# The output stage of a recurrent layer in two parts, and a scheduling priority for mixes and clamps

## The chip, the cores and the metric

The kernel runs on one core of a Trainium2 chip. The metric is the device time of one execution in microseconds (us), the median of several runs. One core has five engines that take their instructions in order, each from its own stream: TensorE (PE: matrix products and transposes; its weight loads, PEld, are listed apart), VectorE (DVE), ScalarE (ACT), GpSimd (POOL) and SyncE (SP, which issues transfers). They wait for each other by semaphores. Products are written to PSUM tiles; the other tiles lie in SBUF.

## The reference

Two layers over 2048 tokens of width 1024, in float32. Each layer normalises its input, projects it, runs one token mixer and one small cross-attention to 256 memory tokens, multiplies both by a SiLU gate, projects back and adds. The first layer's mixer is the one at issue here, a recurrence (RWKV-7) over 12 heads of width 64:

```python
z = z + (token_shift(z) - z) * mu
r, k, v, wd, ad = jnp.split(z, ...)
...
def step(state, inp):
    r_t, w_t, k_t, v_t, kk_t, a_t = inp
    sa = jnp.einsum('bhvk,bhk->bhv', state, -kk_t)
    state = state * w_t + sa * (kk_t * a_t) + v_t * k_t
    y_t = jnp.einsum('bhvk,bhk->bhv', state, r_t)
...
y = ((y - mean) * lax.rsqrt(var + LNX_EPS)) * lnx_w + lnx_b
y = (y + bonus) * silu(gate)
```

(The broadcasts are left out.) The second layer is a differential attention over all tokens, which takes the rest of the time and which the change does not touch.

## The kernel before

**Tiling.** The first layer (`layer_a`) works in steps. A step takes two heads (128 channels, one of 6 pairs) and a block of 512 tokens (8 chunks of 64). With 6 pairs and 4 blocks there are 24 steps; they run in two halves of the sequence, two blocks to a pair's weights. Within a step the recurrence is solved chunk by chunk, with a triangular inverse.

**The stages of a step** (class `Step`):

- `p1`: the projections of k, r and v (`pj`, 24 products each of 128x512), the low-rank decay and rate (`lr`, 4 products), each followed by ScalarE and VectorE work. `mix` (L274 to L279) forms the token shift out of a projection's PSUM bank: a scaled copy on ScalarE, two multiply-adds on VectorE (L277, L278), and a copy of the last column to `carry` (L279). The clamps (L320 for decay and rate) keep an exponential finite. `pss` (L335) sums the squared keys over a head; it needs kx's projection, its mix, kk (L331) and rn (L333).
- `p2`: the masked score matrices (`pg` into `Gm`, L371 and L373), transposes of keys and values (`bkp`, `pvt`), the bonus.
- `p3`: on VectorE, the inverse of 16x16 blocks (30 small operations, L418 and L420), then two block transposes that give T16 (L427) and TT16 (L431).
- `p3b`: the inverse of 64x64 blocks on TensorE: two sets of 32 small products `inv` (L446), the first from E1 and T16, the second from ScalarE's copy of the first (L448) and TT16; then L449 and a block transpose Ta (L452) on VectorE, `invz` (L459), a copy on ScalarE (L461), `invr` (L465), and copies on VectorE (L467).
- `p4`: `atp`, `nvp`, `txp`, `mrp` and `ch`, products with copies on ScalarE between them.
- `p4b`: the chain over the 8 chunks: one product `ch` and one ScalarE copy S for each chunk (L541, L542), with the outputs `yp`, copied to `ys` (L557).
- `p5`: the output stage: statistics and normalisation of `ys` on VectorE (L564 to L575), four transposes `py` on TensorE (L578), a scaled copy on ScalarE (L580), the bonus added on VectorE (L581), the gate multiplied on GpSimd (L582), and a store to `y_dram` on GpSimd's own queue (L583).
- `gate`: the gate's projection and its SiLU (`gate_silu`, L281 to L289), with a clamp on VectorE (L285).

**The order written in the loop.** For step i: p2 and p3 of step i+1, p4b and p5 of step i, p3b and p4 of step i+1, then `filler(i + 2)`, which is the gate of step i+1 and p1 of step i+2, with the loads of weights where they are due.

**What makes the order on an engine.** The order in which the code issues instructions is their rank, not their order. A scheduler places each instruction at build time, by its own estimates of durations: whenever an engine is free, it gives it the instruction of highest rank among those that are ready. The streams that come out are fixed; at run time each engine takes its own in order and waits where the estimate was too short. The projections of the next step, issued last, are so the filling between the products of the current step. `tc.high_priority()` gives what is issued inside it a rank ahead of everything else.

**PSUM.** `ppj` has 3 banks, tag `pj`, for projections, `lr`, `pss` and `pbn`. `pps` has 3 banks, tag `gm`, that serve `pg`, `bkp`, `pvt`, `yp`, `py`, `inv`, `invz`, `invr`, `atp`, `nvp`, `txp` and `mrp` in turn, and 2 for `ch`.

Of the kernel before, what the change touches and what calls it, by code (L numbers as in the profile page):

```python
# [11 lines left out]
ALU = mybir.AluOpType  # L12
# [13 lines left out]
TB = 512  # L26
# [10 lines left out]
BIG = float(2.0 ** 60)  # L37
# [22 lines left out]
def hybrid_kernel(ctx, tc, S, HALF, x, mem, pv, cv, dist, postn, w_out, w_mkv, a_w, w2, a2, w_kv, b_w, out):  # L60
# [4 lines left out]
    V = nc.vector  # L65
# [143 lines left out]
    def layer_a(ph):  # L209
# [43 lines left out]
        def PS(shape, name, tag="gm", bufs=3):  # L253
            if tag == "pj":
                return ppj.tile(shape, F32, name=name, tag="pj", bufs=3)
            return pps.tile(shape, F32, name=name, tag=tag, bufs=bufs)
# [17 lines left out]
        def mix(ps, col, o):  # L274
            m = pc("mu", col)
            A.activation(o, ps, AF.Copy, scale=omu[:, col:col + 1])
            V.scalar_tensor_tensor(out=o[:, 1:TB], in0=ps[:, 0:TB - 1], scalar=m, in1=o[:, 1:TB], op0=ALU.mult, op1=ALU.add)  # L277
            V.scalar_tensor_tensor(out=o[:, 0:1], in0=carry[:, col:col + 1], scalar=m, in1=o[:, 0:1], op0=ALU.mult, op1=ALU.add)  # L278
            V.tensor_copy(out=carry[:, col:col + 1], in_=ps[:, TB - 1:TB])  # L279

        def gate_silu(ps, g, eng=G_):  # L281
            A.activation(g, ps, AF.Copy)  # L282
            e = W([P, TB], "e_sil")
            A.activation(e, g, AF.Exp, scale=-1.0)
            V.tensor_scalar(out=e, in0=e, scalar1=BIG, scalar2=None, op0=ALU.min)  # L285
            A.activation(e, e, AF.Ln, bias=1.0)
            A.activation(e, e, AF.Exp, scale=-1.0)
            eng.tensor_tensor(out=g, in0=g, in1=e, op=ALU.mult)
            return g  # L289
# [13 lines left out]
        class Step:  # L303
# [5 lines left out]
            def p1(self):  # L309
                p, h, th, ws = self.p, self.h, self.th, self.ws  # L310
                lora = self.lora
                cum = W([P, NC, 65], "cum")
                asg = W([P, TB], "asg")
                G_.memset(cum[:, :, 0:1], 0.0)
                for i, e in enumerate((cum[:, :, 1:65], asg.rearrange("p (c t) -> p c t", t=C))):
                    pl = PS([P, TB], "lr", "pj")
                    mm(pl, lhsT=lora[:, i], rhs=th[i], start=True, stop=False)
                    mm(pl, lhsT=lora[:, 2 + i], rhs=th[i], start=False, stop=True)
                    A.activation(e, pl.rearrange("p (c t) -> p c t", t=C), AF.Exp, bias=nwa[:, i * 6 + p:i * 6 + p + 1], scale=-1.0)
                    V.tensor_scalar(out=e, in0=e, scalar1=BIG, scalar2=None, op0=ALU.min)  # L320
                    A.activation(e, e, AF.Ln, bias=1.0)
                    A.activation(e, e, AF.Exp, scale=-1.0)
                kx = W([P, TB], "kx")
                mix(pj(ws[0], h), 6 + p, kx)
                cumf = cum.rearrange("p c t -> p (c t)")
                V.tensor_tensor_scan(cumf, cc("smask", NC * 65), cumf, 0.0, op0=ALU.mult, op1=ALU.add)
                Pt = W([P, NC, 65], "Pt")
                A.activation(Pt, cum, AF.Exp, scale=-DEC)
                A.activation(cum, cum, AF.Exp, scale=DEC)
                kk = W([P, TB], "kk")  # L330
                V.tensor_scalar(out=kk, in0=kx, scalar1=pc("k_k", p), scalar2=None, op0=ALU.mult)  # L331
                rn = W([P, TB], "rn")
                A.activation(rn, kk, AF.Square)  # L333
                pss = PS([P, TB], "pss", "pj")
                mm(pss, lhsT=bones, rhs=rn, start=True, stop=True)  # L335
                V.tensor_scalar(out=rn, in0=pss, scalar1=1e-12, scalar2=None, op0=ALU.max)
                A.activation(rn, rn, AF.Ln)
                A.activation(rn, rn, AF.Exp, scale=-1.0)
                G_.tensor_tensor(out=rn, in0=rn, in1=asg, op=ALU.mult)

                AR = T([P, NC, P], "AR", 2)
                BK = TL([P, NC, P], "BK", 1)
                Pt4 = Pt.rearrange("p (j e) t -> p j e t", e=2)
                Pi4 = cum.rearrange("p (j e) t -> p j e t", e=2)[:, :, :, 1:65]
                V.tensor_tensor(out=slots(AR, True), in0=q4(kk), in1=Pt4[:, :, :, 0:64], op=ALU.mult)
                G_.tensor_tensor(out=kk, in0=kk, in1=rn, op=ALU.mult)
                V.tensor_tensor(out=slots(BK, True), in0=q4(kk), in1=Pi4, op=ALU.mult)

                V.tensor_scalar(out=asg, in0=asg, scalar1=pc("k_a", p), scalar2=oka[:, p:p + 1], op0=ALU.mult, op1=ALU.add)
                G_.tensor_tensor(out=kx, in0=kx, in1=asg, op=ALU.mult)  # L350
                V.tensor_tensor(out=slots(BK, False), in0=q4(kx), in1=Pi4, op=ALU.mult)
                PC = T([P, NC], "PC", 3)
                V.tensor_copy(out=PC, in_=Pt[:, :, 64])
                rx = W([P, TB], "rx")
                mix(pj(ws[1], h), p, rx)
                V.tensor_tensor(out=slots(AR, False), in0=q4(rx), in1=Pt4[:, :, :, 1:65], op=ALU.mult)
                G_.tensor_tensor(out=kx, in0=rx, in1=kx, op=ALU.mult)
                vx = W([P, TB], "vx")
                mix(pj(ws[2], h), 12 + p, vx)
                self.rk, self.AR, self.BK, self.PC, self.vx = kx, AR, BK, PC, vx  # L360

# [195 lines left out]
                    A.activation(ys[:, :, hh], py[hh], AF.Copy)  # L557

            def p5(self):
                p, ys, sil = self.p, self.ys, self.sil  # L560
                bs = T([P, 8, 6], "bs", 1)
                y8 = ys.rearrange("p j h v -> p (j h) v")
                for i in range(8):
                    V.bn_stats(out=bs[:, i, :], in_=y8[:, i, :])  # L564
                sm = T([P, 4, 8], "sm", 1)
                V.tensor_tensor(out=sm[:, 0], in0=bs[:, :, 1], in1=bs[:, :, 4], op=ALU.add)
                V.tensor_tensor(out=sm[:, 1], in0=bs[:, :, 1], in1=bs[:, :, 4], op=ALU.subtract)
                V.tensor_tensor(out=sm[:, 2], in0=bs[:, :, 2], in1=bs[:, :, 5], op=ALU.add)
                V.scalar_tensor_tensor(out=sm[:, 3], in0=sm[:, 1], scalar=16.0, in1=sm[:, 1], op0=ALU.mult, op1=ALU.mult)
                V.tensor_tensor(out=sm[:, 2], in0=sm[:, 2], in1=sm[:, 3], op=ALU.add)  # L570
                V.tensor_scalar(out=sm[:, 0], in0=sm[:, 0], scalar1=0.5, scalar2=None, op0=ALU.mult)
                A.activation(sm[:, 3], sm[:, 2], AF.Ln, bias=eps_t[:, 1:2], scale=1.0 / 64)
                A.activation(sm[:, 3], sm[:, 3], AF.Exp, scale=-0.5)
                V.tensor_tensor(out=y8, in0=y8, in1=sm[:, 0, :, None].broadcast_to([P, 8, 64]), op=ALU.subtract)
                V.tensor_tensor(out=y8, in0=y8, in1=sm[:, 3, :, None].broadcast_to([P, 8, 64]), op=ALU.mult)  # L575
                py = PS([P, NJ, P], "py")
                for j in range(NJ):
                    nc.tensor.transpose(py[:, j, :], ys[:, j].rearrange("p h v -> p (h v)"), ident)  # L578
                yo = ys.rearrange("p j h v -> p (j h v)")
                A.activation(yo, py.rearrange("p j t -> p (j t)"), AF.Identity, bias=pc("lnx_b", p), scale=pc("lnx_w", p))  # L580
                V.tensor_tensor(out=yo, in0=yo, in1=self.bon, op=ALU.add)  # L581
                G_.tensor_tensor(out=yo, in0=yo, in1=sil, op=ALU.mult)  # L582
                G_.dma_start(out=y_dram[p * P:(p + 1) * P, self.t0:self.t0 + TB], in_=yo)  # L583
# [109 lines left out]
        for i in range(n):  # L693
            if i + 1 < n:
                steps[i + 1].p2()
                steps[i + 1].p3()
            steps[i].p4b()
            if i == n - 1:
                load_wo(0)
                for m in range(2):  # L700
                    mem_q(m, NHALF - 1, [NB - 1], ws[m])
                stl.close()
                op = OutProj(0, y_dram, x, x1_dram, 3)
            steps[i].p5()
            if i + 1 < n:
                steps[i + 1].p3b()
                steps[i + 1].p4()
            if i + 2 <= n:
                filler(i + 2)
            if i == n - 2:  # L710
                ws = [mem_w(m) for m in range(2)]
                for m in range(2):
                    mem_q(m, NHALF - 1, range(NB - 1), ws[m])
# [610 lines left out]
```

## Time and profile before

| | us |
|---|---|
| median of 3 runs | 3177.18 (3177.15 to 3179.72) |
| the profiled execution | 3178.13 |
| its span, first to last instruction | 3176.3 |
| TensorE busy | 2965.9 (93% of the span) |
| VectorE busy | 1792.0 (56%) |
| ScalarE busy | 1508.2 (47%) |
| GpSimd busy | 873.6 (28%) |

The span holds the whole program; 1.8 us of the profiled execution lie outside it. The busy shares are means over both layers. The first layer's steps end at some 1500 us. Of the rows further down, those of the order of time give the start, the duration, the engine, the line, the operation and, in brackets, how long the engine stood idle before it and what released it. A row of matrix products shows how many are merged (x32), and a tile's name is cut at the first digit of its number, so that T16 reads T and TT16 reads TT.

### The profile page before, as it was taken

The numbers are of one execution on the slowest core, as the hardware profiler recorded it, in microseconds if no ns is written. First come the engines' busy times: TensorE is split into PE (matmuls) and PEld (weight loads), VectorE is DVE, ScalarE is ACT, GpSimd is POOL, SyncE is SP. The second block draws the span as 40 slices with busy tenths as digits, with TensorE's granted clock in tenths as the row PEclk, the third lists the DMA queues.
The fourth block names the chain that finished last, engine by engine and source line by source line (L and its number), as shares of the span: only waits on it lengthen the run. The fifth ranks groups of instructions, "written<-read, shape, count | busy, mean of one in ns | idle before, by whom it ended". The sixth has DMA issues, their size and how long they took to land.

```text
span 3176.3 us, 57448 instructions
## 1 busy us (share of the span) xinstructions
PE 2965.9 (93%) x22378; PEld 2401.6 (76%) x22378; DVE 1792.0 (56%) x4728; ACT 1508.2 (47%) x3318; POOL 873.6 (28%) x936
## 2 busy tenths in 40 slices
PE   6889999998789999998899999999999999998999
PEld 4667777776667777777677798898887787786777
DVE  6566767655656676764465311101108888887554
ACT  5535454444444544444455422313216777776343
POOL 3133433442134334431000222412312223222100
PEclk8999999998789999999999999999999999999999
DMA  3211000122110001103554523423454556533453
GB/s 118 80 30 36 28 23 26 35 77 79 36 33 28 23 26 33 38 25 86 164 145 126 155 80 99 118 83 87 117 158 110 114 112 120 116 80 108 121 156 115
DMA packets 266160, 265.45 MB, mean 84 GB/s; under 512 B 16832, under 2 KB 206656, under 8 KB 265760
## 3 DMA queue, kind: packets, MB, share of 16 engines
q1 hardware_dynamic: 237760, 195.31, 21.0%
q0 software_dynamic: 28128, 66.46, 10.3%
q8 instruction: 176, 2.88, 0.4%
q14 instruction: 96, 0.79, 0.1%
HBM read 180.45 MB, written 81.26 MB: 82 GB/s over the span
## 4 chain that ended last, share of the span: by engine, by line
PE 71%; DVE 13%; ACT 8%; issue 3%; DMA 3%; POOL 1%; SPq 1%; ACTq 0%; DVEq 0%; POOLq 0%
PE pj L174 28%; PE po L866 10%; PE o L1179 5%; PE vps L1042 4%; PE s L1138 3%; PE s L1139 2%; PE tr L1169 2%; DMA wraw<-in_a_w 2%; PE inv L446 2%; PE yp L555 1%; PE ch L541 1%; PE mo L805 1%; DVE E L1141 1%; PE mpt L798 1%; PE pss L335 1%
## 5 line engine op out<-in xcount | busy, mean ns | idle before, releaser
L174 PE MATMUL pj<-hhi,wh 128*128 128x512 f32 x928 | 396.3, 427 | 7.8 <-ACT sil L282 2.6
L174 PE MATMUL pj<-hhi,wl 128*128 128x512 f32 x928 | 379.4, 409 | 1.3 <-POOL wl L123 1.3
L174 PE MATMUL pj<-hlo,wh 128*128 128x512 f32 x928 | 373.9, 403 | 0.2 <-DVE hlo L149 0.2
L123 POOL TENSOR_TENSOR wl<-wraw,wh 128x512 fp32r<-128x512 f32 x168 | 220.0, 1320 | 431.5 <-ACT wh L122 378.0
L1141 DVE CUSTOM_DVE_ANT_0 E<-s,dist 128x512 f32<-128x512 f32 (+1 forms) x480 | 276.0, 604 | 35.2 <-PE s L1139 29.0
L174 PE MATMUL pj<-bh,wh 128*128 128x512 f32 x672 | 262.4, 391 | 0.0
L174 PE MATMUL pj<-bh,wl 128*128 128x512 f32 x672 | 262.3, 390 | 0.0
L174 PE MATMUL pj<-bl,wh 128*128 128x512 f32 x672 | 262.2, 390 | 0.0
L1146 ACT ACTIVATE E<-E,nm 128x1920 f32<-128x1920 f32 (+7 forms) x192 | 229.4, 1199 | 59.0 <-DVE nm L1144 58.6
L174 PEld LDWEIGHTS pj<-hhi,wh 128*128 128x128 f32 x928 | 179.2, 193 | 64.7 <-ACT sil L282 8.9
L122 ACT ACTIVATE wh<-wraw 128x512 fp32r<-128x512 f32 x168 | 105.2, 627 | 231.3 <-PE pj L174 143.6
L1179 PE MATMUL o<-th,vs 128*128 128x256 f32 (+1 forms) x864 | 210.9, 376 | 2.4 <-ACT th L1172 0.9
L174 PEld LDWEIGHTS pj<-hlo,wh 128*128 128x128 f32 x928 | 179.7, 194 | 41.7 <-issue 6.8
L174 PEld LDWEIGHTS pj<-hhi,wl 128*128 128x128 f32 x928 | 178.6, 192 | 42.0 <-POOL wl L123 2.2
L1138 PE MATMUL s<-ks,qd 128*128 128x512 f32 (+1 forms) x480 | 205.7, 432 | 2.2 <-DVE mx L1141 1.2
L1179 PEld LDWEIGHTS o<-th,vs 128*128 128x128 f32 x864 | 153.9, 189 | 38.5 <-ACT th L1172 19.2
L1139 PE MATMUL s<-ks,qd 128*128 128x512 f32 (+1 forms) x480 | 176.2, 373 | 0.0
L174 PEld LDWEIGHTS pj<-bh,wh 128*128 128x128 f32 x672 | 126.6, 188 | 26.3 <-DVE ot L877 0.3
L174 PEld LDWEIGHTS pj<-bh,wl 128*128 128x128 f32 x672 | 126.5, 188 | 26.3
L174 PEld LDWEIGHTS pj<-bl,wh 128*128 128x128 f32 x672 | 126.5, 188 | 25.9
L764 POOL DMA_DIRECT2D mq<-mq x64 | 33.3, 526 | 376.0 <-PE ms L783 368.3
L1172 ACT ACTIVATE th<-tr 128x512 f32<-128x512 f32 (+1 forms) x216 | 113.2, 568 | 44.2 <-PE tr L1169 43.8
(416 smaller groups left out, 7112.1 us busy)
## 6 DMA issues: line engine op xcount, KB each, us to landing
wraw<-in_a_w SPq DMA_DIRECT2D x126, 256.0 KB, 2.9
qd<-qd_d POOLq DMA_DIRECT2D x48, 512.0 KB, 7.0
mq<-mq POOLq DMA_DIRECT2D x64, 256.0 KB, 4.3
ks<-ks_d POOLq DMA_DIRECT2D x24, 512.0 KB, 7.2
yr<-y_dram SPq DMA_DIRECT2D x31, 384.0 KB, 5.0
xt<-in_x SPq DMA_DIRECT2D x16, 512.0 KB, 5.3
x_dram<-ot SPq DMA_DIRECT2D x16, 512.0 KB, 4.2
wraw<-in_b_w SPq DMA_DIRECT2D x32, 256.0 KB, 3.1
```

The source lines that it names most:

```text
L122: A.activation(hi[:, ks], raw, AF.Copy)
L123: eng.tensor_tensor(out=lo[:, ks], in0=raw, in1=hi[:, ks].bitcast(F32), op=ALU.subtract)
L174: mm(ps, lhsT=w[a_][:, k, wcol], rhs=h[b_][:, k, tsl], start=n == 0, stop=n == 3 * KT - 1)
L446: mm(pb[rows, j, hh, :], lhsT=lt[rows, j, hh, :], rhs=rt_[rows, j, hh, :], start=True, stop=True)
L866: mm(po[hf], lhsT=a_[:, k, :], rhs=b_[hf][:, k, :], start=k == i == 0, stop=k == KT - 1 and i == 2)
L1042: mm(ps[:, t, :], lhsT=hT[b][a_][:, k, tsl], rhs=w[b_][:, k, :], start=n == 0, stop=n == 3 * KT - 1)
L1138: mm(ps[:, f:f + w_], lhsT=qd[:, 0, c, qs], rhs=k_[:, c, 0:w_], start=True, stop=False)
L1139: mm(ps[:, f:f + w_], lhsT=qd[:, 1, c, qs], rhs=k_[:, c, 0:w_], start=False, stop=True)
L1141: V.tensor_tensor_reduce(out=e[:, kb * 512:kb * 512 + w], in0=ps[:, 0:w], in1=dt_[:, u0:u0 + w], scale=-SLOPES[h], scalar=3.0e38, op0=ALU. ...
L1146: A.activation(E[c][:, 0:nk], E[c][:, 0:nk], AF.Exp, bias=nm[:, c:c + 1], scale=-1.0, accum_out=nm[:, 2 + c:3 + c])
L1172: A.activation(th[:, 0:w], ps[:, 0:w], AF.Copy)
L1179: mm(po[:, oc], lhsT=vs[kt // 4][:, kt % 4, :], rhs=th[:, rc], start=n == 0, stop=n >= nmm - 2, skip_group_check=True)
```

## The change

The output stage is cut in two: `p5` keeps the statistics and the normalisation, `p5b` takes the transposes, the scaled copy, the bonus, the gate and the store. In the loop `p5b` of step i is issued behind `p3b` of step i+1 and ahead of its `p4`; in the last step it follows `p5` as before. Besides, the VectorE part of `mix` and the clamps in `gate_silu` and `p1` are issued under high priority. No instruction is added or taken away.

```diff
             A.activation(o, ps, AF.Copy, scale=omu[:, col:col + 1])
-            V.scalar_tensor_tensor(out=o[:, 1:TB], in0=ps[:, 0:TB - 1], scalar=m, in1=o[:, 1:TB], op0=ALU.mult, op1=ALU.add)
-            V.scalar_tensor_tensor(out=o[:, 0:1], in0=carry[:, col:col + 1], scalar=m, in1=o[:, 0:1], op0=ALU.mult, op1=ALU.add)
-            V.tensor_copy(out=carry[:, col:col + 1], in_=ps[:, TB - 1:TB])
+            with tc.high_priority():
+                V.scalar_tensor_tensor(out=o[:, 1:TB], in0=ps[:, 0:TB - 1], scalar=m, in1=o[:, 1:TB], op0=ALU.mult, op1=ALU.add)
+                V.scalar_tensor_tensor(out=o[:, 0:1], in0=carry[:, col:col + 1], scalar=m, in1=o[:, 0:1], op0=ALU.mult, op1=ALU.add)
+                V.tensor_copy(out=carry[:, col:col + 1], in_=ps[:, TB - 1:TB])
...
             A.activation(e, g, AF.Exp, scale=-1.0)
-            V.tensor_scalar(out=e, in0=e, scalar1=BIG, scalar2=None, op0=ALU.min)
+            with tc.high_priority():
+                V.tensor_scalar(out=e, in0=e, scalar1=BIG, scalar2=None, op0=ALU.min)
...
-                    V.tensor_scalar(out=e, in0=e, scalar1=BIG, scalar2=None, op0=ALU.min)
+                    with tc.high_priority():
+                        V.tensor_scalar(out=e, in0=e, scalar1=BIG, scalar2=None, op0=ALU.min)
...
                 V.tensor_tensor(out=y8, in0=y8, in1=sm[:, 3, :, None].broadcast_to([P, 8, 64]), op=ALU.mult)
+
+            def p5b(self):
+                p, ys, sil = self.p, self.ys, self.sil
                 py = PS([P, NJ, P], "py")
...
             steps[i].p5()
             if i + 1 < n:
                 steps[i + 1].p3b()
+                if True:
+                    steps[i].p5b()
                 steps[i + 1].p4()
+            if False or i + 1 == n:
+                steps[i].p5b()
             if i + 2 <= n:
                 filler(i + 2)
```

## Rows read from the trace of the kernel before

**Rows 1.** The page's first part: busy time, share of the span, instructions.

```profile
PE 2965.9 (93%) x22378; PEld 2401.6 (76%) x22378; DVE 1792.0 (56%) x4728; ACT 1508.2 (47%) x3318; POOL 873.6 (28%) x936
```

**Rows 2.** Busy time by stretch: length, engines, granted clock, DMA share, GB/s.

```profile
190.00:665.00 475.00, 442.34 (x5029) 352.21 (x5029) 328.24 (x866) 225.07 (x491) 182.76 (x181) 0.99 0.09 27
665.00:1030.00 365.00, 316.09 (x2779) 248.93 (x2776) 205.73 (x534) 166.09 (x382) 123.06 (x114) 0.88 0.19 54
1030.00:1502.00 472.00, 443.95 (x4885) 355.51 (x4884) 305.75 (x818) 218.33 (x479) 168.10 (x163) 0.99 0.13 38
```

**Rows 3.** TensorE's waits, 50 to 1420 us: total us, times, longest us.

```profile
PE py L578 <- DVE ys L575: 18.3, 19, 1.3
PE pg L371 <- DVE carry L279: 13.2, 14, 1.7
...
PE pss L335 <- ACT rn L333: 11.6, 4, 4.3
PE txp L504 <- ACT X L495: 8.7, 18, 0.5
PE mrp L519 <- ACT UV L507: 7.8, 22, 0.4
...
PE inv L446 <- DVE T L427: 6.9, 4, 4.0
...
PE invz L459 <- DVE Ta L452: 5.1, 10, 2.0
```

**Rows 4.** One step in order of time, TensorE: start, duration, what, idle before.

```profile
399.61 0.50 PE L174 MATMUL pj<-hhi,wh 128*128 128x512 f32 x1 [0.27 <-ACT sil L282]
...
403.25 0.63 PE L578 MATMUL py<-cvt,ys 128*128 128x128 f32 x4 [1.31 <-DVE ys L575]
403.81 1.15 PE L446 MATMUL inv<-T,E 64*64 64x64 f32 x32
...
411.05 0.73 PE L465 MATMUL invr<-TT,Ta 32*32 32x32 f32 x32
411.71 1.09 PE L485 MATMUL atp<-cvt,AR 128*64 128x128 f32 x16
...
417.92 1.15 PE L530 MATMUL ch<-UV,BKT 128*64 128x64 f32 x32
419.00 1.13 PE L335 MATMUL pss<-rn,cvt 128*128 128x512 f32 x2
...
453.61 0.63 PE L578 MATMUL py<-cvt,ys 128*128 128x128 f32 x4 [0.87 <-DVE ys L575]
```

**Rows 5.** The same step in order of time, VectorE.

```profile
379.26 0.68 DVE L356 TENSOR_TENSOR AR<-rx,Pt 128x512 f32<-128x512 f32 x1
...
398.41 1.07 DVE L427 STREAM_TRANSPOSE T<-X 128x512 f32<-128x512 f32 x1
...
401.24 1.06 DVE L431 STREAM_TRANSPOSE TT<-X 128x512 f32<-128x512 f32 x1
402.16 0.94 DVE L575 TENSOR_TENSOR ys<-ys,sm 128x512 f32<-128x512 f32 x1
403.02 0.41 DVE L285 TENSOR_SCALAR e_sil<-e_sil 128x512 f32<-128x512 f32 x1
...
413.82 0.48 DVE L331 TENSOR_SCALAR kk<-kx,pvt 128x512 f32<-128x512 f32 x1
```

**Rows 6.** The chain that ended last, the r and v projections.

```profile
420.12 10.92 PE pj L174 x48
```

**Rows 7.** Lines L349 and L582: ns min/median/max, first and last start.

```profile
L349 DVE TENSOR_SCALAR asg<-asg,pvt,oka x24: 543/1619/1629, 65.0 to 1412.3; 128x512 f32<-128x512 f32 x24
...
L582 POOL TENSOR_TENSOR ys<-ys,sil x24: 1261/1292/2147, 194.1 to 1504.2; 128x512 f32<-128x512 f32 x24
```

**Rows 8.** The same step in order of time, ScalarE.

```profile
411.16 0.69 ACT L276 ACTIVATE kx<-pj,omu 128x512 f32<-128x512 f32 x1
...
414.48 0.63 ACT L333 ACTIVATE rn<-kk 128x512 f32<-128x512 f32 x1
```

More of the change, by code (lines that the diff above doesn't have):

```diff
@@ L559, in p5 @@
             def p5(self):
-                p, ys, sil = self.p, self.ys, self.sil
+                ys = self.ys
                 bs = T([P, 8, 6], "bs", 1)
```

## The prediction

> **What bounds the kernel now.** I read the page first, for which engine is full, then the busy time by stretch, then TensorE's waits over the first layer, then one step of that layer in order of time. TensorE is the bound: 93% busy [rows 1]. The first layer runs as 24 steps. In its two even stretches a step takes some 50 us (py starts at 403.25 and again at 453.61 [rows 4]), TensorE is busy 442 of 475 us and 444 of 472 us, and its granted clock is 0.99, so nearly all of it at the 2.4 GHz level [rows 2]. Between them lies the change of halves, with 49 us of 365 idle at clock 0.88 [rows 2]. So only TensorE's holes can be won: 32.7 us of 475, or 3.4 us in each 50.
>
> The waits say what the holes are [rows 3]: the transposes py wait for VectorE's last normalising multiply (18.3 us in 19 waits, 0.96 each), pg for the masks and mixes, pss for the squared keys, txp and mrp for ScalarE's copies, inv and invz for VectorE's transposes. One step shows the place [rows 4, 5]. T16 is ready at 398.41 + 1.07 = 399.48 us, and with E1, long finished, that is all that the first inverse product needs; yet it starts at 403.81, straight behind py, which stood 1.31 us waiting for ys (402.16 + 0.94). In those four microseconds TensorE ran projection matmuls, the lowest rank of all, and then nothing. So readiness did not hold it. Every PSUM tile of this chain comes from one pool of three banks, and they are given out in program order: atp needs only AR, finished at 379.94, and still starts at 411.71, straight behind invr [rows 4, 5]. I read from this that inv is held back by py's place in that order. That is the one inference on which the forecast rests.
>
> **The change, part by part.**
>
> *py behind the inverse.* Program order in the pool becomes inv, inv, invz, invr, py, atp. The py wait goes: ys is ready at 403.1, and py's new turn, behind invr, comes at some 408 even if the inverse runs four microseconds earlier. Removed: up to 18.3 us [rows 3]. The four transposes, the scaled copy, the add, the gate multiply on GpSimd and its one store on GpSimd's queue are the same instructions, some 5 us later. Nobody waits for them within the layer: y rows are read back by the output projection, and in the last step the order is as before. I cost this at zero; the cover is that whole layer, and without it the one store would cost a few microseconds once.
>
> *The inverse earlier.* TensorE comes free at 399.61 - 0.27 = 399.34 [rows 4], T16 is there at 399.48: some 0.2 us of wait, in the place of the 0.27 that it spends there for sil. I take 0.2 x 19 = 4 us; the other bound is the four waits for T at 6.9 us, 1.7 each [rows 3]. The second product needs TT16, ready at 401.24 + 1.06 = 402.30. The clamps now go ahead of it (below). The order on TensorE is fixed at build from estimated durations; that py waits 0.96 us on average says that VectorE runs this far behind the estimate at that point. So a wait of 0 to 0.96 us is to be expected at inv for TT16; I take the middle, 0.48 x 19 = 9 us. invz waits 5.1 us in all now [rows 3]; with VectorE's lag already paid at inv I count that as gone. Sum of this part: -18.3 - 5.1 + 4 + 9 = -10.4 us, between -23.4 (no new wait) and 0 (the same lag paid elsewhere).
>
> *The inverse's tail.* Behind invr stand atp, nvp, txp, mrp, ch, pss. There the waits of txp and mrp are 8.7 and 7.8 us [rows 3], since no projection matmul is to be had: the next one must follow pss in its own pool of three banks, and pss needs kx's projection, its mix, kk and rn. Left-over kx matmuls could fill these holes (-16.5 us at most), or end so late that pss waits (the rival below). Estimate: 0, as the inverse's own gaps still take most of kx's 24 matmuls, 24 x 10.92 / 48 = 5.5 us [rows 6].
>
> *Priority for the mixes and clamps.* No instruction is added; on VectorE, whichever of these is ready goes first. In the step shown e_sil's clamp runs at 403.02 and takes 0.41 us [rows 5], and the step has two more of its size; ahead of TT16 the three would put TT16 and ys back by up to 1.2 us, which py's new place covers and inv's second product partly does not; that is why I did not take the lower bound above. The banks that mixes empty are not what TensorE waits for in the steady steps: no wait for a bank's mix stands among the projection's own [rows 3], and pg's 13.2 us end with the mix of vx and the masks, where the mix already goes first. Gain 0 to 2 us; I take 1.
>
> *GpSimd beside VectorE.* The same kind of VectorE operation, a 128x512 multiply-add in SBUF, takes 543 ns at best and 1619 ns in the median [rows 7] where a GpSimd operation is under way. The gate multiply (1292 ns in the median) moves from beside inv to beside kk, 0.48 us long now [rows 5, 7], on the way to pss. By these rows pss is ready up to 1.08 us later; TensorE has other work until 419.00 while rn is ready at 415.11 [rows 4, 8], so 0 in the sum. The Trainium skill, SBUF — State Buffer, section on the two physically separate sides, says the pair of ports that the two engines share is an exclusive lock held for a whole instruction, the loser fully blocked. The stretched row agrees; by the rule alone the sum would be the same and only the rival below dearer by that microsecond.
>
> Sum: -10.4 - 1 = -11 us. The profiled execution took 3178.13 us, its span 3176.3; that is 0.95 over the median of 3177.18, so the same difference goes on the median: **3166 us**.
>
> **Rivals.**
>
> *The lag moves, nothing is won.* VectorE is as far behind its estimate at T16, TT16 and Ta as at ys, and inv and invz pay what py paid. For it: four times inv waits for T itself, 1.7 us each, so there it was VectorE's lag and not py that held it [rows 3]. Against it: T16 is within 0.2 us of TensorE in the steady step. Time: 3177, give or take 5. The case that the pool does not hold inv back at all, so that the order hardly changes, ends here too.
>
> *All of it is won.* No wait at inv, and kx's matmuls fill half of the holes of txp and mrp: -23.4 - 8 = -31, so 3146 us. For it: TensorE has the filler just there. Against it: each of these orders rests on estimates that are already 1 us out.
>
> *Slower: kx ends too late.* The inverse takes rank over kx's projection. From ScalarE's copy of kx (411.16) to rn (414.48 + 0.63) are 3.95 us [rows 8], now covered by 7.95 us of TensorE work between invr and pss (411.05 to 419.00) [rows 4]. Each kx matmul that falls behind invr, atp or nvp shortens that cover, and nothing else can run, because the next projection stands behind pss. It decides from the point where under 3.95 us of work lie between kx's last matmul and pss. If the last falls behind mrp, ch alone is left, 1.1 us until pss [rows 4]: a wait of 2.85 us, 3.9 with the stretched kk. The trace has such waits: pss for rn, 11.6 us over 4 steps [rows 3]. Less what is won (0.96 for py, 0.9 for the filled holes of txp and mrp) that is 1.0 to 2.1 us a step; x 19 it is 19 to 40, say 3200 us. Against it: the inverse's chain of copies leaves TensorE free for most of kx's 5.5 us before invr.
>
> **How the numbers follow.** Forecast (part of the wait won) 0.40, all won 0.18, the lag moves 0.24, kx too late 0.18. What a measurement of this kernel can tell from no change is about 0.2%, 6.4 us: below 3170.8 is faster, above 3183.5 slower. Faster: 0.38 of the forecast case and all of the second, 0.56. Same: 0.22 of the third case and 0.02 of the forecast, 0.24. Slower: 0.18 and 0.02 of the third, 0.20. The stretch between the halves, where orders may change in ways I can't follow, adds some 5 us either way. The range takes in the case of all won and half of the slow one: 3143 to 3196. The forecast case alone would be 3157 to 3172.
>
> **What would show it.** Right: on TensorE the first inverse product stands ahead of py, right behind the lr matmuls; py stands behind invr with no wait; the py row of the waits is gone and inv has new waits for T or TT of under half its size; the clamps stand ahead of TT16 on VectorE. The even stretches shrink by some 0.5 us a step, and all else, the second layer above all, keeps its length. Wrong: inv waits for T and TT by as much as py did (the lag moves); pss waits for rn in most steps (slower); py still ahead of inv (the inference on the pool fails); or the time changes between 665 and 1030 us by more than in the even stretches.

## The result: slower by 0.67%, and the profile after

The changed kernel took 3198.04 us (median of 4 runs, 3191.41 to 3201.79) against 3177.16 us for the kernel before beside it: ratio 1.0067, 95% interval 1.0044 to 1.0089. The forecast was 3166, the range ended at 3196, and slower had a chance of 0.20. The profiled execution has a span of 3195.7 us, 19.4 more than before.

TensorE's waits in the first layer, changed kernel, 50 to 1450 us (total us, times, longest us; behind the edits line numbers are up to ten higher than before):

```profile
PE ch L544 <- ACT S L545: 31.0, 42, 2.7
PE inv L449 <- DVE X L432: 20.2, 9, 2.2
PE pss L338 <- ACT rn L336: 15.9, 13, 4.2
PE pg L374 <- DVE Gm L376: 11.3, 15, 1.7
...
PE pg L374 <- DVE carry L280: 7.9, 9, 1.7
...
PE inv L449 <- DVE T L430: 5.8, 11, 3.0
```

Against [rows 3] the waits of py and invz are gone and that of txp nearly so. New is inv for X, 20.2 us (inv for T had 6.9 and has 5.8); ch for S was 12.4 us before, and pss is up from 11.6 to 15.9. So waits were exchanged for fewer and longer ones.

That alone is not the loss. The next two fences cut the first layer at the starts of steps, so that the work in a row is the same in both kernels: eight steps, the stretch between the halves, nine steps. First the kernel before, then the changed one (length, busy us and instructions of TensorE, weight loads, VectorE, ScalarE and GpSimd, granted clock of TensorE, DMA share, GB/s):

```profile
233.49:639.00 405.51, 379.19 (x4291) 302.87 (x4290) 279.45 (x746) 191.97 (x420) 160.55 (x157) 0.99 0.10 29
639.00:971.45 332.45, 286.73 (x2459) 225.44 (x2457) 184.31 (x484) 153.54 (x352) 106.16 (x101) 0.87 0.19 54
971.45:1425.53 454.08, 425.04 (x4818) 338.76 (x4817) 314.86 (x838) 216.06 (x471) 182.17 (x178) 0.99 0.10 30
```

```profile
232.59:651.42 418.83, 388.48 (x4291) 308.15 (x4290) 280.68 (x746) 191.91 (x420) 160.74 (x157) 0.96 0.09 28
651.42:970.60 319.18, 280.21 (x2451) 219.78 (x2450) 181.01 (x484) 152.39 (x348) 106.19 (x101) 0.89 0.20 56
970.60:1445.38 474.78, 438.37 (x4833) 347.07 (x4832) 319.19 (x839) 218.30 (x478) 184.62 (x179) 0.96 0.10 29
```

The 17 steps take 13.3 + 20.7 = 34.0 us more. Idle time of TensorE (length less busy) is 30.35 + 36.41 us against 26.32 + 29.04, so 11.4 of the 34.0. The other 22.6 us are busy time, for the same 4291 matmuls in the first row: they take longer on average, and the granted clock is 0.96 in place of 0.99. The stretch between the halves gives 13.3 us back, half of it idle time and half busy time at a clock of 0.89 in place of 0.87. All else, the second layer among it, makes the remaining -1.3 us: 34.0 - 13.3 - 1.3 = 19.4.

**The even-block step** of the changed kernel, TensorE from ch to pss, and then ScalarE beside it:

```profile
364.68 1.15 PE L533 MATMUL ch<-UV,BKT 128*64 128x64 f32 x32
365.76 0.50 PE L174 MATMUL pj<-hhi,wh 128*128 128x512 f32 x1
...
367.71 0.39 PE L174 MATMUL pj<-hhi,wl 128*128 128x512 f32 x1
367.94 0.33 PE L544 MATMUL ch<-sb,MT 128*128 128x64 f32 x2
369.90 0.43 PE L544 MATMUL ch<-S,MT 128*128 128x64 f32 x2 [1.63 <-ACT S L545]
370.74 0.43 PE L544 MATMUL ch<-S,MT 128*128 128x64 f32 x2 [0.41 <-ACT S L545]
371.77 1.12 PE L338 MATMUL pss<-rn,cvt 128*128 128x512 f32 x2 [0.60 <-ACT rn L336]
...
368.45 0.67 ACT L276 ACTIVATE kx<-pj,omu 128x512 f32<-128x512 f32 x1
...
371.10 0.62 ACT L336 ACTIVATE rn<-kk 128x512 f32<-128x512 f32 x1
```

Nine of kx's 24 matmuls fall behind ch. kx's copy starts at 368.45, rn ends at 371.72, and pss starts right there, 3.3 us behind the copy's start, where 7.8 us lay between the two before [rows 4, 8]. Three pairs of the recurrence's ch fill a little of the time and wait for S themselves: 2.64 us idle in all, 0.60 of it ahead of pss. Most of the wait stands in the list under ch, but what holds TensorE is kx: with kx's projection put first, further down, these waits of 1.63 us are gone.

**The odd-block step** after it, around the first inverse product:

```profile
399.44 0.69 DVE L578 TENSOR_TENSOR ys<-ys,sm 128x512 f32<-128x512 f32 x1
...
400.79 1.29 POOL L123 TENSOR_TENSOR wl<-wraw,wh 128x512 fp32r<-128x512 f32 x1 [4.67 <-PE lr L320]
400.91 2.73 DVE L428 TENSOR_SCALAR X<-Ti,cvt 128x256 f32<-128x256 f32 x2
...
402.08 1.32 POOL L123 TENSOR_TENSOR wl<-wraw,wh 128x512 fp32r<-128x512 f32 x1
...
403.67 1.04 DVE L430 STREAM_TRANSPOSE T<-X 128x512 f32<-128x512 f32 x1
...
404.57 0.28 DVE L432 TENSOR_SCALAR X<-Ti,cvt 128x256 f32<-128x256 f32 x1
...
404.86 1.97 PE L449 MATMUL inv<-T,E 64*64 64x64 f32 x32 [2.24 <-DVE X L432]
409.19 1.97 PE L449 MATMUL inv<-TT,E 64*64 64x64 f32 x32
...
415.06 0.72 PE L468 MATMUL invr<-TT,Ta 32*32 32x32 f32 x32
415.71 0.66 PE L584 MATMUL py<-cvt,ys 128*128 128x128 f32 x4
```

The order is the one forecast: inv ahead of py, py behind invr without a wait. But ys's normalisation now runs on VectorE ahead of the last steps of Ti, and the two copies X (L428), which took 0.73 us together in the other steps, meet two weight splits of GpSimd and take 2.73. T16 is 2 us late, and inv waits 2.24 us. (The profile names X of L432, which came last before 404.86; the transpose T that ends at 404.71 is what inv reads.) The Trainium skill, SBUF — State Buffer, section on its two separate sides, says that a VectorE operation in one of its two-port modes and a GpSimd operation take a shared pair of ports as a lock, whichever starts first, for a whole instruction. The row agrees, 2.73 us beside GpSimd and 0.73 alone; that X runs in such a mode no row here shows.

**Behind the hole** the inverse products take 1.97 us each; before they took 1.15 [rows 4]. The changed kernel around 404.86, by stretches of 5 us:

```profile
400.00:405.00 5.00, 2.69 (x13) 1.61 (x14) 4.83 (x10) 3.31 (x6) 2.61 (x3) 0.92 0.07 19
405.00:410.00 5.00, 5.00 (x52) 3.94 (x54) 1.99 (x5) 3.70 (x7) 1.93 (x3) 0.50 0.20 60
410.00:415.00 5.00, 4.89 (x66) 3.68 (x64) 2.17 (x3) 0.82 (x3) 0.00 (x0) 0.90 0.01 3
```

From 405 to 410 the granted clock is 0.50, the 1.2 GHz level, and TensorE is fully busy. The same stretches of the kernel before are all at 1.00. Counted over 190 to 660 and 1030 to 1420 us, the kernel before has one hole of over 1.5 us (4.01 at inv, 199 us) and none in the 17 steps; the changed one has 17, and at 12 of them the clock fell. A hole of that size is not needed, though: in the 17 steps of the kernel before the clock fell four times, each time right behind a wait of pg of 1.0 to 1.2 us (granted 0.50 from 281.4 to 284.8 behind 1.17 us), and not once behind the eight waits of py of 1.3 us.

### The profile page after: what moved, and what is told of

It is laid out like the page before. It is cut to its first block, busy times and chain, and to the rows that moved or that the text cites. A ratio compares the mean times of both kernels' runs of the same rounds, so it can differ in the third digit from the quotient of the medians.

```text
span 3195.7 us, 57441 instructions
## 1 busy us (share of the span) xinstructions
PE 2983.3 (93%) x22378; PEld 2411.4 (75%) x22378; DVE 1793.3 (56%) x4728; ACT 1508.1 (47%) x3318; POOL 873.6 (27%) x936
## 5 line engine op out<-in xcount | busy, mean ns | idle before, releaser
L174 PE MATMUL pj<-hhi,wh 128*128 128x512 f32 x928 | 403.6, 435 | 4.6 <-DVE hlo L149 1.4
```

The costliest lines, as they stand in the source:

```text
L174: mm(ps, lhsT=w[a_][:, k, wcol], rhs=h[b_][:, k, tsl], start=n == 0, stop=n == 3 * KT - 1)
```

## The experiments

Fourteen kernels in four questions. The table gives for most of them the time, the ratio to the kernel before with its interval (that kernel was measured anew beside them, with medians of 3173.62 to 3178.36 us), and the row of the same eight steps (steps 2 to 9, 4290 or 4291 matmuls): length, busy, idle (their difference) and granted clock.

| kernel | us | ratio | steps | busy | idle | clock |
|---|---|---|---|---|---|---|
| before | 3177.16 | 1 | 405.51 | 379.19 | 26.32 | 0.99 |
| after | 3198.04 | 1.0067 [1.0044, 1.0089] | 418.83 | 388.48 | 30.35 | 0.96 |
| split only | 3198.08 | 1.0078 [1.0063, 1.0094] | 418.37 | 386.99 | 31.38 | 0.97 |
| priority only | 3195.34 | 1.0066 [1.0052, 1.0079] | 420.00 | 393.50 | 26.50 | 0.96 |
| mixes' priority only | 3174.51 | 1.0002 [0.9992, 1.0011] | 405.12 | 379.24 | 25.88 | 0.99 |
| clamps' priority only | 3200.38 | 1.0079 [1.0060, 1.0098] | 417.04 | 389.04 | 28.00 | 0.97 |
| after, p5b behind p4 | 3235.50 | 1.0188 [1.0163, 1.0214] | 437.86 | 396.21 | 41.65 | 0.94 |
| after, rx first | 3200.37 | 1.0082 [1.0068, 1.0095] | 424.36 | 394.20 | 30.16 | 0.95 |
| after, X on ScalarE | 3191.66 | 1.0052 [1.0040, 1.0065] | 419.48 | 388.63 | 30.85 | 0.97 |
| before, X on ScalarE | 3148.29 | 0.9915 [0.9902, 0.9928] | 395.41 | 377.46 | 17.95 | 1.00 |
| split only, X on ScalarE | 3203.26 | 1.0091 [1.0075, 1.0106] | 418.78 | 386.34 | 32.44 | 0.98 |
| the same, kx first | 3177.74 | 0.9987 [0.9974, 1.0000] | 412.47 | 384.84 | 27.63 | 0.97 |
| priority only, X on ScalarE | 3153.44 | 0.9917 [0.9903, 0.9930] | 397.92 | 379.15 | 18.77 | 1.00 |

### Which part of the change loses?

**Split only**: p5b as in the change, no priority.

```diff
+            def p5b(self):
...
+                if True:
+                    steps[i].p5b()
                 steps[i + 1].p4()
```

> The split alone, without any priority. Theory (the inverse taking rank over kx's projection makes kx end too late in one step of two, and in the other the output stage's multiplies get ahead of the inverse's on VectorE, so that X stands beside GpSimd's weight split and T16 comes 2 us late): both holes come from the split, so they stay; 3190 to 3200 us, inv waits for VectorE some 20 us in all and pss and ch for ScalarE some 45. Rival (the priority is what does it: clamps and mixes ahead of T16): without it the time is that of my first forecast, 3160 to 3172, and X takes its 0.73 us for two everywhere.

3198.08 us, in the theory's range. The largest of TensorE's waits, 50 to 1450 us, are those of the changed kernel (inv's stand under one name here):

```profile
PE ch L541 <- ACT S L542: 31.0, 42, 2.7
PE inv L446 <- DVE T L427: 27.0, 21, 3.0
```

**Priority only**: the three `with tc.high_priority()` of the change, p5b called in p5's old place.

> The priority alone, with the output stage whole and in its old place. Theory: the clamps put ys back by up to 1 us, so py waits a little longer than before (18.3 us in the 19 waits); 3175 to 3190 us, X takes 0.73 us for two, no new wait at pss. Rival (priority does it): 3195 or more, with the long X and the waits of inv for VectorE.

3195.34 us: the theory's range is missed, the rival's time is met, but X takes 0.73 us here, so its mechanism is not. The waits (50 to 1450 us) add up to much the same as before [rows 3], with pg's longer and py's shorter:

```profile
PE pg L374 <- DVE Gm L376: 21.7, 21, 1.7
PE py L584 <- DVE ys L578: 15.4, 18, 1.4
PE pss L338 <- ACT rn L336: 12.5, 8, 4.2
```

Yet the eight steps are 14.5 us longer, with 0.2 us more idle time and 14.3 more busy time for one matmul less. This is the plainest reading of the study: the sum of the waits is the same and the time is not. (In the nine later steps it is 2.0 us of idle and 5.8 of busy time.) One of pg's waits, 1.71 us in place of 1.03 in the same step before, and the stretches around it:

```profile
386.64 2.05 PE L374 MATMUL pg<-AR,BK 64*128 64x128 f32 x24
390.40 2.06 PE L374 MATMUL pg<-AR,BK 64*128 64x128 f32 x8 [1.71 <-DVE Gm L376]
```

```profile
385.00:390.00 5.00, 3.69 (x32) 2.95 (x30) 2.24 (x3) 1.72 (x3) 3.58 (x3) 1.00 0.31 82
390.00:395.00 5.00, 4.60 (x17) 3.87 (x18) 4.04 (x7) 1.20 (x2) 1.65 (x2) 0.54 0.35 98
395.00:400.00 5.00, 5.00 (x56) 3.82 (x54) 3.83 (x15) 1.81 (x4) 1.47 (x2) 0.77 0.00 0
```

**Clamps only, mixes only**: the kernel before with one kind of priority each.

> The kernel before with priority for the three clamps alone (silu's and the two gates'), not for the mixes. The priority for mixes and clamps together cost 22 us. Theory (the mixes do it: kx's mix and kk go ahead of the copies for the recurrence, and pg and pss find other gaps): with the clamps alone 3170 to 3182. Rival (the clamps do it: they run ahead of TT16 and ys): 3190 or more, with py's wait over 18 us.

> The kernel before with priority for the mixes alone, not for the clamps. The clamps alone took 3200 us, mixes and clamps together 3195. Theory (the clamps make all of that loss): 3170 to 3182, the order on VectorE nearly as before. Rival (each of the two alone moves pg's wait to 1.7 us, and the clock falls behind it): 3190 or more, pg's waits over 21 us.

3200.38 and 3174.51 us. The clamps make the whole loss and the mixes do nothing measurable. With the clamps py's wait is 15.9 us, not over 18 as the rival had it: what the clamps move is pg's wait, from 1.0 to 1.2 us up to 1.71 or more in eight of the 17 steps. The two halves of the change do not add up: the split alone, the clamps alone and both together each cost 21 to 25 us, so on top of the split the priority shows no effect.

### Does moving the second half elsewhere help?

**p5b behind p4**, the priority kept:

```diff
-                if True:
-                    steps[i].p5b()
                 steps[i + 1].p4()
-            if False or i + 1 == n:
-                steps[i].p5b()
+            steps[i].p5b()
```

> The changed kernel with the second part of the output stage behind p4 instead of between p3b and p4. Theory: the place of py behind the inverse matters little, since nobody waits for it; the inverse still takes rank over kx, so both holes stay; within 6 us of the changed kernel, 3190 to 3204. Rival (py, its copy and the gate multiply between invr and nvp are what delays p4): 10 us or more faster than the changed kernel, below 3188.

3235.50 us, which neither range holds: the place of the second half does matter. pss waits 31.6 us and ch 29.0, and the clock of the eight steps is the lowest of all, 0.94.

**rx's projection issued ahead of pss**, so that TensorE has work while it waits for rn:

```diff
+                prx = pj(ws[1], h)
                 pss = PS([P, TB], "pss", "pj")
...
-                mix(pj(ws[1], h), p, rx)
+                mix(prx, p, rx)
```

> The changed kernel with rx's projection issued ahead of pss, so that TensorE has 24 matmuls to do while kx is mixed. Theory: the waits of pss for rn, and those of ch for S that fill the same hole, go (some 40 us of waits between 200 and 1420 us, of which about 25 are the new ones); the long X stays; 3165 to 3185 us. Rival (the hole is only where VectorE's lag shows, not kx's lateness): the waits move to another tile and the time stays above 3190.

3200.37 us, not the theory's 3165 to 3185 but the rival's, and the waits did move to another tile. pss no longer waits, and ch waits 7.5 us only; the long X, which the theory left in place, is gone from all steps but one as well. But everything behind pss is late, and pg pays in each step (waits, 50 to 1450 us):

```profile
PE pg L375 <- DVE BK L355: 64.7, 23, 3.9
```

Holes were moved, not filled.

### Is it the collision at X?

**The changed kernel, and the kernel before, with the masked copy X2 on ScalarE**:

```diff
-                    V.tensor_scalar(out=X2[:, :, ib, :].rearrange("p i t -> p t i"), in0=Ti, scalar1=m01[:, ib:ib + 1], scalar2=None, op0=ALU.mult)
+                    A.activation(X2[:, :, ib, :].rearrange("p i t -> p t i"), Ti, AF.Copy, scale=m01[:, ib:ib + 1])
```

> The changed kernel, with the one multiply that fills X2 ahead of T16 put on ScalarE instead of VectorE. Theory (in every second step VectorE and GpSimd collide at the masked copies X just ahead of T16, the copies take 2.7 us instead of 0.7, TensorE waits 2.2 us for the inverse and its clock falls): the inverse's waits for X (20.2 us) and for T (5.8 us) fall under 8 us in all, the half-clock time in the two even stretches falls from 72 to about 40 us, and the time is 3170 to 3188. Rival (the other holes, ch for S and pss for rn, bring the clock down as well; the collision only adds its own wait): 3188 to 3196, half-clock time 60 us or more.

3191.66 us, the rival's range. The big wait at inv is gone (waits, 50 to 1450 us):

```profile
PE ch L544 <- ACT S L545: 31.0, 42, 2.7
PE pss L338 <- ACT rn L336: 15.5, 13, 4.3
PE inv L449 <- DVE T L430: 14.8, 22, 3.2
```

but inv still waits 0.5 us in every step, and kx's hole and the falls behind it remain. The time at half clock in the two even stretches, by the clock records of the traces, fell from 72 to 41 us, as the theory and not the rival had it. Yet the steps gained nothing: the eight take 419.48 us against 418.83, and the nine behind the change of halves take 474.06 against 474.78, with the same busy time, which the clock alone does not explain:

```profile
964.86:1438.92 474.06, 438.62 (x4832) 346.48 (x4831) 311.16 (x820) 229.85 (x496) 179.60 (x178) 0.97 0.10 29
```

The 6 us between the medians lie between the halves (313.66 us against 319.18), and the two intervals overlap. So the collision is a hole of the changed kernel, but taking it out by this edit does not win its time back.

> The kernel before with the same multiply on ScalarE. Here T16 is ready 4 us before TensorE comes to the inverse, but VectorE is late at ys, for which py waits 18.3 us. Theory (VectorE's chain of copies up to ys sets py): 0.36 us less work on VectorE in each of 23 steps takes up to 8 us from py's wait: 3160 to 3172. Rival (ScalarE's chain from sil to the normalisation gets later by as much, or the holes only move): 3172 to 3185.

3148.29 us, 0.85% faster than the kernel before and 1.6% faster than the changed one, better than the theory said. py's wait (50 to 1450 us) and the eight steps:

```profile
PE py L578 <- DVE ys L575: 5.3, 12, 1.4
```

```profile
232.69:628.10 395.41, 377.46 (x4291) 300.61 (x4290) 279.40 (x730) 200.29 (x436) 162.65 (x157) 1.00 0.10 30
```

Two copies of VectorE fewer in each step (730 instructions in place of 746) take 8.4 us of idle time and 1.7 us of busy time out of eight steps. This is what the change was to win, with the written order left as it was: VectorE was late at ys, and here it is hardly late. Not all of it is the two copies: the pair X ahead of TT16, which met a GpSimd split in every second step before and stands ahead of ys's last multiply [rows 5], takes 0.53 us in the same place here. Before:

```profile
399.34 1.38 DVE L429 TENSOR_SCALAR X<-Ti,cvt 128x256 f32<-128x256 f32 x2
```

### Is it kx, and is it the clock?

**Split only, X on ScalarE**, and the same with **kx's projection first**:

```diff
-                mix(pj(ws[0], h), 6 + p, kx)
+                with tc.high_priority():
+                    pk = pj(ws[0], h)
+                mix(pk, 6 + p, kx)
```

> The output stage in two parts, without the priority, and X2 on ScalarE: against the kernel before with X2 on ScalarE alone (3148 us) it is the split and nothing else, without the collision ahead of T16. Theory (with the split kx's projection ends too late in every second step, ch and pss wait there 2.2 to 2.8 us, and the clock falls behind that hole): 3180 to 3195, idle time per steady step 3.5 us or more against 2.37, half-clock time in the even stretches 40 us or more against 24. Rival (the collision was the split's only loss, and the priority made the rest): 3145 to 3165.

> The split alone with X2 on ScalarE (3203 us), and priority for the 24 matmuls of kx's projection, so that none of them falls behind ch. Theory (the split loses through kx's late end: 55 us against 3148): the waits of ch for S (31 us in 42) fall under 20, those of pss for rn (15.6 us in 13) under 12 us, no hole of over 1.6 us stands ahead of pss, half-clock time in the even stretches falls from 58 to under 35 us, and the time is under 3185. Rival (kx's matmuls are then missing as filler between the inverse's copies, and the holes stand there instead): the waits of inv, invz and invr rise by more than ch's and pss's fall, and the time is 3195 or more.

3203.26 us: without the collision the split costs 55 us against 3148.29, more than the theory said; the eight steps have 14.5 us more idle and 8.9 us more busy time. With kx first 3177.74 us, so 25.5 of the 55 come back (33 of 56 by the ratios). The waits of the two (50 to 1450 us), split first:

```profile
PE ch L541 <- ACT S L542: 31.0, 42, 2.7
PE pss L335 <- ACT rn L333: 15.6, 13, 4.2
```

```profile
PE inv L448 <- ACT E L450: 34.1, 21, 4.0
PE pss L337 <- ACT rn L335: 19.5, 14, 4.6
...
PE ch L543 <- ACT S L544: 8.0, 21, 1.1
```

Part of each side came true. ch's wait falls to 8.0 and the time is under 3185; but the inverse's own gap, 34.1 us for E, opens as the rival said, because kx's matmuls and kx's copy on ScalarE now stand ahead of it, and the clock stays at 0.97. The rival's sum did not come: inv, invz and invr together wait 10 us more, ch and pss 19 us less. (Of pss's 19.5 us 7.6 lie in the first two steps and 8.5 in two steps between the halves; in a steady step it is 0.3.) So kx's late end makes about half of the split's loss there, the price of mending it already taken off, which is the filler that the inverse then lacks. What makes the other half is not shown.

**Priority only, X on ScalarE**:

> The kernel before with X2 on ScalarE (3148 us) and the priority for mixes and clamps, no split. Theory (the clamps ahead of the copies make pg's hole 1.7 us and pss's wait, whatever X does, and the clock falls behind pg): idle time per steady step up by 0.2 to 0.6 us only, half-clock time in the even stretches from 24 to 45 us or more, time 3163 to 3180. Rival (the loss came of the clamps' collision with TT16 and ys, where VectorE now has room): 3145 to 3155, half-clock time under 30 us.

3153.44 us, the rival's range: where VectorE has room, the clamps' priority costs 5 us by the medians and nothing by the ratios (0.9917 and 0.9915), in place of 22, and the clock of the eight steps is 1.00.

**Holes made on purpose.** The fill and the doubled masks were to show the clock by itself, and do so only in part.

```diff
+                    if rt_ is T16 and (self.t0 // TB) % 2:
+                        for _ in range(NFILL):
+                            mm(pb.rearrange("p j h t -> p (j h t)")[:, 0:256], lhsT=ident, rhs=self.Ti.rearrange("p a b -> p (a b)"), start=True, stop=True)
```

> The changed kernel with ten products of 128x256 whose result is thrown away put ahead of the first inverse product in the 12 steps on an odd block: some 2.75 us of TensorE work in each at the full clock, 33 us in all, standing where TensorE waits 26 us for X and T. Rival (only the waits count): 33 of work less at most 26 of wait is +7 us, so 3205 or more. Theory (a hole of two microseconds here costs more than itself, because the granted clock falls behind it): half-clock time in the two even stretches falls by 30 us or more, which gives back at least 12 us at the 0.4 us each that the steps measured so far show: 3180 to 3195, in spite of more work.

3273.27 us (1.0311 [1.0297, 1.0324]): not the theory's, and far above the sum of 3205 from which the rival's range starts. The result of these products is overwritten by the first real one. The loop runs twice in a step, so 20 products stand there and not ten: 220 between 190 and 1502 us, 51.7 us of busy time, 4.7 in each of 11 steps. ch's waits rise from 31.0 to 48.9 us. It says that more work at that place is no cure; of the clock it says nothing, as the order changed with it.

```diff
                     for hh in range(2):
+                        for _ in range(2 if e == hh == 0 else 1):
...
```

> The kernel before with X2 on ScalarE (3148 us, 24 us of half-clock time in the two even stretches, pg's waits 1.07 and 0.60 us in turn), and the first of the four mask multiplies done twice, so that the bank for which pg waits comes free 0.68 us later in each step. Rival (a wait costs itself): at most 24 x 0.68 = 16 us, so 3155 to 3165 with TensorE's busy time per step as before (47.2 us). Theory (a hole of that size also brings the granted clock down behind it, at 0.37 us of busy time for each us at half clock): pg's wait is 1.7 us in every second step, half-clock time in the even stretches rises to 45 us or more, busy time per step to 47.8 or more, and the time is 3168 to 3182.

> As the last one, with that multiply done three times: the bank comes free 1.36 us later. Rival (a wait costs itself): at most 24 x 1.36 = 33 us, 3170 to 3181, busy time per step 47.2 us. Theory (the clock falls as well): pg waits 2.4 and 1.9 us in turn, the clock falls in most steps, half-clock time in the even stretches 70 us or more, busy time per step 48.4 or more, time 3190 to 3215.

The loop has the range 2 in the first kernel, 3 in the second. With the multiply done twice 3246.09 us (1.0233 [1.0214, 1.0253]), with three 3172.35 us (0.9996 [0.9985, 1.0006]): more added work, less time. The order on each engine is fixed at build from estimated durations, and the two builds chose different ones. In the first the pair X ahead of TT16 (L430) meets GpSimd, 2.19 us, and the inverse waits more; in the second they do not meet in the steady steps. The eight steps, doubled and then tripled:

```profile
235.12:673.53 438.41, 396.38 (x4290) 313.46 (x4289) 288.33 (x737) 200.36 (x437) 154.45 (x157) 0.95 0.09 27
```

```profile
237.54:641.63 404.09, 377.05 (x4290) 300.54 (x4289) 294.06 (x746) 200.69 (x437) 158.70 (x157) 0.99 0.10 29
```

Neither theory foresaw the first. The second is the rival's: 9.1 us more idle time than at 3148 us and no more busy time, although inv waits 2.6 us in every second step. Of its eight holes of that size in the 17 steps, five were followed by a fall of the clock.

Over all kernels with the same matmuls in the eight steps their busy time goes with the granted clock: 377.05 to 379.24 us at 0.99 or 1.00, 384.84 to 396.38 at 0.94 to 0.98. Idle time does not decide it alone (26.50 and 26.32 us of idle go with 393.50 and 379.19 busy). An estimate from the table: with the levels 1.00 and 0.50, a mean clock of 0.96 over 420.00 us is some 34 us at the lower level, and 0.99 over 405.51 some 8; the priority alone has thus 26 us more at that level, for 14.3 us more busy time. That TensorE is slower at the lower level is shown by the stretches above, and the falls of the changed kernel stand at its holes. Which holes bring one about is not settled: 1.71 us did in one kernel, 1.89 us did not in the kernel at 3148 us, and 1.17 us did in the kernel before where 1.31 us did not. No run changed the clock with the order left as it was.

## Why the prediction was wrong

The step that failed is the price of what comes in the place of py's wait: 0 for the tail, 13 us for inv, and nothing for the clock. What was to go did go, and more: in the 17 steps the waits of py, invz, txp and for sil fell by 31 us. But inv waits 20.3 us there in place of 0.8, ch and pss 25.0 in place of 1.4, and the same matmuls take 22.6 us more.

*The pool holds inv back.* Right: with py moved, inv stands behind lr (in every second step behind five matmuls of kx as well), py behind invr and without a wait; 18.3 us of py's and 5.1 of invz's are gone, as summed.

*"So a wait of 0 to 0.96 us is to be expected at inv".* Wrong in size and place: 4 us were put down for T16 and 9 for TT16; all of the 20.3 us came at T16, and for TT16 inv never waits. That is as much as py's wait was there (17.6 us), which the prediction had named as a sign of being wrong, but not for the reason that it gave with it. The lag of VectorE was taken from py's wait in the old order; in the new one ys's normalisation goes ahead of Ti, and the copies X move beside GpSimd's splits. The prediction weighed GpSimd for the gate's multiply only, which it watched moving, and not for what stays in place and meets other neighbours.

*"Estimate: 0" for the inverse's tail.* Wrong: in every second step nine matmuls of kx end behind ch. This is the slower rival, and its time (3200) was right, but by luck: it put 1.0 to 2.1 us on 19 steps, and the trace has 2.64 us in every second one; the rest of that time is the clock's, which it did not price. The rows of before that it called on are no such waits: the four of pss for rn, and three of the four of inv for T (4.0 us the longest), lie outside the 17 steps.

*"Gain 0 to 2 us; I take 1" for the priority.* Not borne out: on top of the split it shows no gain (ratio 1.0067 with it, 1.0078 without, the intervals overlap), and alone it costs 22 us (1.0066), all of it from the clamps. Their cost was seen (1.2 us ahead of TT16 and ys) as one of waits; alone the waits hardly grow in sum, and what grows is the busy time.

*The sum as a whole.* Each term was a wait, priced at its own length, at the 2.4 GHz level that the even stretches had. Of 34.0 us lost in 17 steps only 11.4 are waits; 22.6 are matmuls at the lower level. The kernel before had no hole of over 1.5 us in these steps: with the priority alone, fewer and larger holes of the same sum in the eight steps cost 14.3 us more busy time. The rows at 0.99 and, between the halves, at 0.88 [rows 2] stood in the prediction, but the second was read as a fact of that stretch and not as what waits do to the clock.

*"Some 5 us either way" between the halves.* It gave 13.3 us back. Without that the result would have been near 3211. How the orders changed there was not followed.

## What to carry to other kernels

Where TensorE is over 90% busy at its full clock, look at the largest holes that an edit makes and not only at the sum of the waits. A large hole need not bring the clock down (eight of 2.6 us left the busy time as it was in one kernel), so compare TensorE's busy time for the same matmuls, cut at the starts of steps: a lower clock shows there and in no list of waits. Where an engine that feeds TensorE is late, take work off it before changing the order: here two small copies a step moved to ScalarE won 27 us (ratio 0.9915), and the change of order lost 21. When an order is written by a builder from estimates, each edit reshuffles operations that it does not touch, so look for those whose duration depends on a neighbour (VectorE beside GpSimd).

## What was not expected of the hardware

The clock falls inside a stretch in which TensorE is 93% busy: granted 0.50 from 405 to 410 us at one hole of 2.24 us, with the engine fully busy in those five. A VectorE copy pair of 0.73 us took 2.73 us beside two GpSimd operations of 1.3 us each. And a kernel with more work on VectorE (three masks, 3172.35 us) was faster than one with less (two masks, 3246.09 us), with another order built for each; no other cause was looked for.
